# Encoder layer on one core: factor kept on chip, half product formed in PSUM, constants in one load, later sums for the second group, operands by halves

## The chip, the cores and the metric

The kernel runs on one core of a Trainium2 chip. The core has a matrix engine (TensorE, PE in the profile), a vector engine (VectorE, DVE), a scalar engine (ScalarE, ACT), GpSimd (POOL) and SyncE (SP), which here issues every DMA, in one queue and in order. Each engine runs its own instructions in the order of the program and waits for the others by semaphores. The metric is the time of one execution on the device in microseconds (us); lower is better.

## The reference

One encoder layer is computed in fp32 on a prompt of 512 tokens and a sample of 1024, with 1024 features: a feed-forward layer, a mixer (half long convolutions, half retention), and another feed-forward layer, each with norms before and after.

```python
def rmsnorm(x, g):
    return x * lax.rsqrt(jnp.mean(x * x, axis=-1, keepdims=True) + NORM_EPS) * g
def swiglu(h, w1, w3, w2):
    return (jax.nn.silu(h @ w1) * (h @ w3)) @ w2

x = x + 0.5 * rmsnorm(swiglu(rmsnorm(x, ffn1_pre_g), w1, w3, w2), ffn1_post_g)
u = rmsnorm(x, mix_pre_g) @ w_in
y_h = hyena_mixer(short_conv(u[..., :1536], short_w, short_b), ...)   # FFT convolutions, two orders
y_r = retention_mixer(u[..., 1536:], ...)
x = x + rmsnorm(concat(y_h, y_r) @ w_out, mix_post_g)
x = x + 0.5 * rmsnorm(swiglu(rmsnorm(x, ffn2_pre_g), w1, w3, w2), ffn2_post_g)
```

## The kernel before, in words

All 1536 tokens pass through each stage, with features on the partitions and tokens along the free axis. Every fp32 matrix product is three matmuls (`mm3`, L67 to L69): each operand is split into a high part, which ScalarE writes (`hi_act`, L59, tiles ending in h), and a low part, which VectorE subtracts (`lo`, L62, tiles ending in l); in the convolution GpSimd forms some of the low parts.

**Feed-forward layers** (0 to about 1050 us and from about 2210 us to the end). Tokens go in two groups g of 768, each in two halves th of 384. `quad` tiles hold 128 partitions x 4 blocks of features x 384 tokens (128x1536); kh is the half of the features. A scheme of seven products per unit takes the place of eight block products: `operands` forms b11, t2, b21, t3, t1, t4 and b22 from the four quarters of the normed input once for each group, and `up_unit`, called for 22 units f, multiplies weight sums with them into the banks ua, ub and uc. `normed` makes the normed input of a half: it loads xq, sums the squares (ScalarE squares, VectorE adds, L158 to L163), multiplies by the gains (L186), has TensorE sum over the partitions (`rstd3`, the bank ss, L172), spreads the factor r over the partitions (`spread`, three transposes into the bank rps, L179), and multiplies (L208). Where the factor is already known it takes another way: a row of factors in HBM is loaded with a broadcast (rq, L205). `post` of the mixer's closing computes that row (r, stored by L588), one `g` of 512 tokens at a time, for the second feed-forward layer.

The second group is made ready beside the units of the first. `ahead` is a generator whose steps the units call, one in the middle of each unit and one behind it: `normed` for both halves, stored to HBM (nx, L469), then sums of the down-projection's weights (`weight_sums`). A step of it contains several instructions, and its place in the program fixes the place of its matmuls in TensorE's order.

**The convolution** (`hyena`, 1715 to about 2125 us). `filter_spectra` transforms the filters (jobs K), `hyena` the signals (jobs Z): transposes into tr banks, `forward` into one bank fw for each block, then the product of the two spectra, complex and block by block, with s the filter's spectrum. It is these four lines, L989 to L992, for 48 blocks of 128x512:

```python
nc.vector.tensor_tensor(p1, ps, a, ALU.mult)
nc.vector.tensor_tensor(p2, ps, s[:, bi:bi + 1].broadcast_to([128, 2, 256]), ALU.mult)
nc.vector.tensor_tensor(p1[:, 0], p1[:, 0], p2[:, 1], ALU.add)
nc.vector.tensor_tensor(p1[:, 1], p1[:, 1], p2[:, 0], ALU.subtract)
```

ps is the fw bank in PSUM, p1 and p2 are in SBUF. ScalarE and GpSimd then split p1 into yh and yl, and the inverse transforms follow. Most jobs have two fw banks in turn (`alt`); the last three (pZ01, pZ10, pZ11) run beside the output projection with one.

**Constants.** `short_consts` loads the short convolution's three weights and its bias at the program's start, as 4 DMAs of single 4-byte elements (L868, L869).

The order of instructions on each engine comes from a scheduler that simulates a timeline when the program is built. The code's order and the generators' steps give it what it orders.

## Time and profile before

| | us |
|---|---|
| median of 3 runs | 3272.43 |
| the 3 runs | 3269.87, 3272.43, 6079.1 |
| the profiled execution | 3269.82 |
| its span in the trace | 3268.0 |
| TensorE busy in the span | 3044.8 (93%) |
| VectorE busy | 2621.3 (80%) |
| ScalarE busy | 1526.9 (47%) |
| GpSimd busy | 507.6 (16%) |

The profiled execution stands 1.8 us above its span and among the two lower runs. The run of 6079.1 is an outlier. Busy shares are averages over stages; idle time of an engine counts where that engine sets the pace of its stage. [...]

### The profile page before, as it was taken

To read this page: it belongs to the slowest core of one execution; us is meant where nothing else is said; L and a number is where in the kernel's file an instruction comes from. 1 tells how busy PE (TensorE), PEld (TensorE's weight loads), DVE (VectorE), ACT (ScalarE), POOL (GpSimd) and SP (SyncE) were. 2 spreads that over 40 slices of the span, in tenths; PEclk is the share of its full clock that TensorE was granted. 3 is DMA by queue.
4 is the path that set the end of the run, shared out by engine and by line. 5 is a ranking of instruction groups with operands and counts; after the bars stand their busy time and mean duration, and the time that the engine had idled before them with its cause. 6 is when DMAs were issued, how large, how long until landed. Compare 5 with 4: busy or idle time off the path is not lost. (4 is left out here: it accounts for less than half of the span.)

```text
span 3268.0 us, 46298 instructions
## 1 busy us (share of the span) xinstructions
PE 3044.8 (93%) x16766; PEld 2864.0 (88%) x16766; DVE 2621.3 (80%) x4215; ACT 1526.9 (47%) x2607; POOL 507.6 (16%) x368
## 2 busy tenths in 40 slices
PE   5999999999999999989989997996899999999997
PEld 4999999999999777767768886876899999999997
DVE  7888888877787599988767788887789788877776
ACT  6433465433455434457644344454433465433454
POOL 0000000000200112556424445520000000000000
PEclk9999999999999999999999998997899999999998
DMA  4686344422344634454652125474678344322244
GB/s 130 231 299 246 91 149 142 120 72 75 102 129 146 207 113 163 153 191 135 178 163 103 48 93 180 138 225 156 251 261 311 89 150 146 130 70 77 85 130 139
DMA packets 224181, 491.48 MB, mean 150 GB/s; under 512 B 37584, under 2 KB 65744, under 8 KB 221776
## 3 DMA queue, kind: packets, MB, share of 16 engines
q1 hardware_dynamic: 223952, 488.54, 46.0%
q8 instruction: 131, 2.15, 0.3%
q14 instruction: 98, 0.80, 0.1%
HBM read 386.67 MB, written 101.75 MB: 149 GB/s over the span
## 5 line engine op out<-in xcount | busy, mean ns | idle before, releaser
L68 PE MATMUL dn<-xl,w2h 128*128 128x384 f32 x1232 | 414.6, 337 | 6.4 <-DVE xl L62 6.4
L59 ACT ACTIVATE wh<-s 128x512 fp32r<-128x512 f32 x352 | 221.3, 631 | 412.9 <-PE ua L68 115.5
L67 PE MATMUL dn<-xh,w2h 128*128 128x384 f32 x1232 | 402.1, 336 | 1.8 <-ACT xh L59 1.7
L69 PE MATMUL dn<-xh,w2l 128*128 128x384 f32 x1232 | 401.8, 337 | 0.0
L59 ACT ACTIVATE wh<-raw 128x512 fp32r<-128x512 f32 (+1 forms) x316 | 220.7, 698 | 350.2 <-PE ub L68 93.5
L62 DVE TENSOR_TENSOR wl<-s,wh 128x512 fp32r<-128x512 f32 x352 | 241.3, 686 | 155.7 <-ACT wh L59 85.5
L59 ACT ACTIVATE w2h<-raw 128x512 fp32r<-128x512 f32 (+1 forms) x340 | 228.1, 672 | 269.7 <-PE dn L68 181.0
L96 POOL TENSOR_TENSOR r<-m,mhalf 128x3 f32<-128x3 f32 (+1 forms) x35 | 41.2, 1179 | 1904.0 <-DVE m L95 1903.1
L62 DVE TENSOR_TENSOR w2l<-raw,w2h 128x512 fp32r<-128x512 f32 (+1 forms) x320 | 225.7, 715 | 93.3 <-ACT w2h L59 78.0
L67 PE MATMUL wips<-hh,wh 128*128 128x512 f32 x576 | 230.8, 401 | 13.1 <-DVE o L812 6.3
L68 PEld LDWEIGHTS dn<-xl,w2h 128*128 128x128 f32 x1232 | 232.3, 189 | 7.2 <-DVE xl L62 7.1
L67 PEld LDWEIGHTS dn<-xh,w2h 128*128 128x128 f32 x1232 | 230.6, 188 | 2.3 <-ACT xh L59 2.0
L69 PE MATMUL wips<-hh,wl 128*128 128x512 f32 x576 | 229.7, 400 | 1.8 <-POOL wl L62 1.7
L69 PEld LDWEIGHTS dn<-xh,w2l 128*128 128x128 f32 x1232 | 231.3, 189 | 0.0
L68 PE MATMUL wips<-hl,wh 128*128 128x512 f32 x576 | 229.5, 399 | 0.0
L62 DVE TENSOR_TENSOR wl<-raw,wh 128x512 fp32r<-128x512 f32 (+1 forms) x280 | 201.4, 719 | 30.7 <-ACT wh L59 29.0
L67 PE MATMUL fw<-th,mh 128*128 128x256 f32 x448 | 132.9, 298 | 26.1 <-DVE spec L951 21.6
L67 PEld LDWEIGHTS wips<-hh,wh 128*128 128x128 f32 x576 | 110.2, 191 | 41.4 <-DVE o L812 6.3
L67 PE MATMUL ub<-t2h,wh 128*128 128x384 f32 x352 | 120.6, 343 | 25.1 <-ACT t2h L59 20.6
L67 PE MATMUL ub<-t4h,wh 128*128 128x384 f32 x352 | 121.2, 344 | 14.9 <-DVE u L279 14.1
L69 PEld LDWEIGHTS wips<-hh,wl 128*128 128x128 f32 x576 | 110.0, 191 | 28.4 <-POOL wl L62 3.1
L68 PE MATMUL fw<-tl,mh 128*128 128x256 f32 x448 | 133.2, 298 | 1.3 <-DVE tl L62 1.2
(386 smaller groups left out, 9075.9 us busy)
## 6 DMA issues: line engine op xcount, KB each, us to landing
raw<-ffn_w SPq DMA_DIRECT2D x440, 256.0 KB, 2.7
raw<-ws SPq DMA_DIRECT2D x220, 256.0 KB, 2.6
wsum<-ffn_w SPq DMA_DIRECT2D x60, 768.0 KB, 6.5
raw<-w_in_f SPq DMA_DIRECT2D x52, 512.0 KB, 4.1
ws<-wsum SPq DMA_DIRECT2D x30, 768.0 KB, 4.6
xq<-x SPq DMA_DIRECT2D x16, 768.0 KB, 5.8
res<-x SPq DMA_DIRECT2D x16, 768.0 KB, 6.0
wsum<-ffn_w SPq DMA_DIRECT2D x20, 512.0 KB, 6.6
```

The source lines that it names most:

```text
L59: self.nc.scalar.activation(hi, src, AF.Copy)
L62: eng.tensor_tensor(lo, src, hi.bitcast(F32), ALU.subtract)
L67: mm(ps, lhsT=ah, rhs=bh, start=first, stop=False, **kw)
L68: mm(ps, lhsT=ah, rhs=bl, start=False, stop=False, **kw)
L69: mm(ps, lhsT=al, rhs=bh, start=False, stop=last, **kw)
L96: nc.gpsimd.tensor_tensor(r, m, self.mhalf[:, :n], ALU.pow)
```

## The change

It has five parts.

1. `short_consts`: the host lays weights and bias side by side as `short`, and one DMA of 128 rows of 48 elements loads them.
2. `ahead`: behind the first step of `normed` (load, squares, sums) of each half of the second group, two more empty steps are yielded. The step with ss comes two half units later, and all steps behind it too.
3. `post`: the factor r is copied to a tile `near` of 128x8 in SBUF; only group 0 still stores its row. `ready` passes `near[:, 3:6]` to `normed` for the second half of the second layer's first group, and `normed` then spreads it by transposes.
4. `normed` multiplies by halves of the features (128x768), the two halves of the features in turn; `operands` forms t1 and t2 by halves, and b11 and t2 are split by halves. t1 is formed behind the load of h22.
5. `hyena`: p2 is formed first; then ps is multiplied by a in place, in PSUM; the add and the subtract read ps and p2 and write p1.

```diff
--- before.py
+++ after.py
@@ -75,6 +75,7 @@
         nc.sync.dma_start(self.ident, self.io["ident"])
         self.mhalf = self.cp.tile([128, 8], F32, name="mhalf")
         nc.gpsimd.memset(self.mhalf, -0.5)
+        self.near = self.cp.tile([128, 8], F32, name="near")
         self.one = ones = self.cp.tile([128, 1], F32, name="ones")
         nc.gpsimd.memset(ones, 1.0)
         self.ones = self.cp.tile([128, 128], F32R, name="onesr")
@@ -201,14 +202,23 @@
             r = self.spread(r)
         else:
             self.gained(xs, gi)
-            r = self.half("rq")
-            nc.sync.dma_start(r, row.broadcast_to([128, 384]))
+            if row.shape[0] == 128:
+                r = self.spread(row)
+            else:
+                r = self.half("rq")
+                nc.sync.dma_start(r, row.broadcast_to([128, 384]))
         yield
-        for x in xs:
-            nc.vector.tensor_tensor(x, x, r.unsqueeze(1).broadcast_to([128, 4, 384]), ALU.mult)
-
-    def split(self, pool, src, name):
+        for k in range(0, 4, 2):
+            for x in xs:
+                nc.vector.tensor_tensor(x[:, k:k + 2], x[:, k:k + 2], r.unsqueeze(1).broadcast_to([128, 2, 384]), ALU.mult)
+
+    def split(self, pool, src, name, halves=False):
         h, l = self.quad(pool, f"{name}h", F32R), self.quad(pool, f"{name}l", F32R)
+        if halves:
+            for k in range(0, 4, 2):
+                self.hi_act(h[:, k:k + 2], src[:, k:k + 2])
+                self.lo(self.nc.vector, l[:, k:k + 2], src[:, k:k + 2], h[:, k:k + 2])
+            return h, l
         self.hi_act(h, src)
         self.lo(self.nc.vector, l, src, h)
         return h, l
@@ -221,13 +231,14 @@
         b = first or {}
         h11, h12 = load(0, 0), load(0, 1)
         if not first:
-            b["11"] = self.split(X, h11, "b11")
+            b["11"] = self.split(X, h11, "b11", True)
         t1 = self.quad(Y, "t1")
-        tt(t1, h12, h11, ALU.subtract)
         yield
         h22, t2 = load(1, 1), self.quad(Y, "t2")
-        tt(t2, h22, t1, ALU.subtract)
-        b["t2"] = self.split(X, t2, "t2")
+        for k in (slice(0, 2), slice(2, 4)):
+            tt(t1[:, k], h12[:, k], h11[:, k], ALU.subtract)
+            tt(t2[:, k], h22[:, k], t1[:, k], ALU.subtract)
+        b["t2"] = self.split(X, t2, "t2", True)
         tt(h12, h22, h12, ALU.subtract)
         yield
         h21 = load(1, 0)
@@ -433,7 +444,7 @@
             return True
 
         def ready(g, th, xs):
-            row = None if row_in is None or g else row_in[:, 384 * th:384 * th + 384]
+            row = None if row_in is None or g else self.near[:, 3:6] if th else row_in[:, :384]
             return self.normed([srcs[g][kh][th] for kh in range(2)], pre, Y, row, xs)
 
         h = [], []
@@ -452,7 +463,7 @@
                     for step in steps:
                         next(step)
                 run(steps[0], 9)
-                first = {"11": self.split(X, h[0][0], "b11")}
+                first = {"11": self.split(X, h[0][0], "b11", True)}
                 run(steps[1], 9)
                 for _ in self.operands(lambda kh, th: h[th][kh], X, Y, first=first):
                     pass
@@ -464,7 +475,11 @@
                 yield from lead
                 for th in range(2):
                     xs = []
-                    yield from ready(1, th, xs)
+                    for i, _ in enumerate(ready(1, th, xs)):
+                        yield
+                        if i == 0:
+                            yield
+                            yield
                     for kh in range(2):
                         nc.sync.dma_start(nx[kh][th], xs[kh])
                     yield
@@ -585,7 +600,9 @@
             for t in range(4):
                 nc.tensor.matmul(ss[:, t:t + 1], lhsT=a2[:, t * 128:(t + 1) * 128], rhs=self.one, start=True, stop=True)
             r = self.rstd(ss, 1.0 / D)
-            nc.sync.dma_start(row[:, 512 * g:512 * g + 512].rearrange("o (c p) -> (o p) c", p=128), r)
+            nc.vector.tensor_copy(self.near[:, 4 * g:4 * g + 4], r)
+            if g == 0:
+                nc.sync.dma_start(row[:, 512 * g:512 * g + 512].rearrange("o (c p) -> (o p) c", p=128), r)
 
     def last_third(self, g, d, src, dst, X, Y):
 
@@ -863,10 +880,7 @@
             yield
 
     def short_consts(self):
-        nc = self.nc
-        for i in range(3):
-            nc.sync.dma_start(self.scw[:, :, i], self.io["short_w"][i])
-        nc.sync.dma_start(self.scw[:, :, 3], self.io["short_b"])
+        self.nc.sync.dma_start(self.scw, self.io["short"])
 
     def mix_in_consts(self, rop):
         self.rope = rop.tile([128, 2, 1024], F32, name="rope", bufs=1)
@@ -986,10 +1000,10 @@
             p2 = ca.tile([128, 2, 256], F32, tag="p2", name="p2", bufs=2)
             a = s[:, 0:2] if last else s[:, 0:1].broadcast_to([128, 2, 256])
             bi = 2 if last else 1
-            nc.vector.tensor_tensor(p1, ps, a, ALU.mult)
             nc.vector.tensor_tensor(p2, ps, s[:, bi:bi + 1].broadcast_to([128, 2, 256]), ALU.mult)
-            nc.vector.tensor_tensor(p1[:, 0], p1[:, 0], p2[:, 1], ALU.add)
-            nc.vector.tensor_tensor(p1[:, 1], p1[:, 1], p2[:, 0], ALU.subtract)
+            nc.vector.tensor_tensor(ps, ps, a, ALU.mult)
+            nc.vector.tensor_tensor(p1[:, 0], ps[:, 0], p2[:, 1], ALU.add)
+            nc.vector.tensor_tensor(p1[:, 1], ps[:, 1], p2[:, 0], ALU.subtract)
             pl = self.c1
             yh = pl.tile([128, 2, 256], F32R, tag=f"yh{i}", name="yh")
             yl = pl.tile([128, 2, 256], F32R, tag=f"yl{i}", name="yl")
@@ -1408,7 +1422,7 @@
     w=g('w_in').reshape(8,128,28,128).transpose(2,1,0,3)
     r['w_in_f']=asc(np.concatenate([w[:20],w[24:]]))
     r['w_in_v']=asc(g('w_in')[:,2560:3072].reshape(4,2,128,512).transpose(0,2,1,3))
-    r['short_w']=asc(g('short_w').reshape(3,12,128).transpose(0,2,1)); r['short_b']=asc(g('short_b').reshape(12,128).T)
+    r['short']=asc(np.concatenate([g('short_w'),g('short_b')[None]]).reshape(4,12,128).transpose(2,1,0))
     for i in '123': r['filt_w'+i]=g('filt_w'+i); r['filt_b'+i]=asc(g('filt_b'+i)[:,None])
     r['filt_freq']=asc(g('filt_freq')[:,None])
     r['filt_w4']=asc(g('filt_w4').reshape(64,16,128).transpose(1,0,2))
```

SyncE's queue at the program's start, before: ident and gains are the identity and the norms' gains, xq a quad of the input, raw a tile of weights, scw the short convolution's constants.

```order
L83 DMA gains<-gains 128x48
L194 DMA xq<-x 128x1536 x2
L250 DMA raw<-ffn_w 128x512 x5
L868 DMA scw<-short_w 128x12x1 x3
L869 DMA scw<-short_b 128x12x1
L194 DMA xq<-x 128x1536 x2
```

After, the same piece:

```order
L84 DMA gains<-gains 128x48
L195 DMA xq<-x 128x1536 x2
L261 DMA raw<-ffn_w 128x512 x5
L883 DMA scw<-short 128x48
L195 DMA xq<-x 128x1536 x2
```

One DMA stands in the place of four, between the first weights and the second half's input.

TensorE in the second feed-forward layer, around the ss of the second group's first half, before: it stands at the border of two units, behind b22, the last of a unit's seven products.

```order
L67 MATMUL uc<-b22h,wh 128x384
L68 MATMUL uc<-b22l,wh 128x384
L69 MATMUL uc<-b22h,wl 128x384
L172 MATMUL ss<-ones,acc 128x1 x3
L67 MATMUL ua<-b11h,wh 128x384
L68 MATMUL ua<-b11l,wh 128x384
L69 MATMUL ua<-b11h,wl 128x384
```

After:

```order
L67 MATMUL ub<-t3h,wh 128x384
L68 MATMUL ub<-t3l,wh 128x384
L69 MATMUL ub<-t3h,wl 128x384
L67 MATMUL uc<-t1h,wh 128x384
L68 MATMUL uc<-t1l,wh 128x384
L173 MATMUL ss<-ones,acc 128x1 x3
L69 MATMUL uc<-t1h,wl 128x384
```

The products with b11, t2, b21 and t3 of the next unit and two matmuls of t1 now stand ahead of ss, 50 matmuls in all; in the first layer it is five products, 60 matmuls.

SyncE's queue at the second feed-forward layer's start, before: row is the row of factors in HBM, z a piece of the output projection's result.

```order
L194 DMA xq<-x_000_82 128x1536
L194 DMA xq<-x_010_84 128x1536
L194 DMA xq<-x_001_83 128x1536
L194 DMA xq<-x_011_85 128x1536
L588 DMA row_91<-r 128x4x1
L624 DMA z_155<-z_21992 128x512
L250 DMA raw<-ffn_w 128x512
L205 DMA rq<-row_91 128x384
L250 DMA raw<-ffn_w 128x512 x8
```

After:

```order
L195 DMA xq<-x_000_83 128x1536
L195 DMA xq<-x_010_85 128x1536
L195 DMA xq<-x_001_84 128x1536
L195 DMA xq<-x_011_86 128x1536
L641 DMA z_156<-z_22023 128x512
L261 DMA raw<-ffn_w 128x512 x9
```

The store of the row and the load of its factors are gone from between the input, the z and the weights.

## Rows read from the trace of the kernel before

**Rows 1.** The page's first part: busy time, share and instructions by engine.
```profile
PE 3044.8 (93%) x16766; PEld 2864.0 (88%) x16766; DVE 2621.3 (80%) x4215; ACT 1526.9 (47%) x2607; POOL 507.6 (16%) x368
```

**Rows 2.** Stretches: length, busy us by engine (instructions), granted clock, DMA share, GB/s.
```profile
1715.00:2125.00 410.00, 365.43 (x2509) 336.58 (x2510) 331.31 (x538) 164.77 (x312) 189.39 (x156) 0.95 0.33 113
2208.00:2260.00 52.00, 25.33 (x100) 21.27 (x99) 37.24 (x44) 26.39 (x38) 3.46 (x2) 0.68 0.38 111
2360.00:3220.00 860.00, 856.82 (x4943) 855.20 (x4943) 685.83 (x1154) 395.41 (x699) 2.98 (x2) 1.00 0.46 146
```

**Rows 3.** Timeline of the start: start, duration, instruction, and the idle time before it.
```profile
5.36 6.16 SPq L868 DMA_DIRECT2D scw<-short_w  x3
...
17.25 1.48 ACT L158 ACTIVATE sq<-xq 128x1536 f32<-128x1536 f32 x1 [3.05 <-DMA xq<-x]
...
43.60 0.69 PE L67 MATMUL ub<-t2h,wh 128*128 128x384 f32 x1 [5.13 <-ACT t2h L59]
```

**Rows 4.** Timeline around the later sums of squares, both feed-forward layers, TensorE and ScalarE.
```profile
79.65 0.99 PE L172 MATMUL ss<-ones,acc 128*128 128x1 f32 x6 [4.21 <-DVE acc L162]
...
2294.98 1.48 ACT L158 ACTIVATE sq<-xq 128x1536 f32<-128x1536 f32 x1 [5.84 <-DMA xq<-x]
...
2306.92 1.44 PE L172 MATMUL ss<-ones,acc 128*128 128x1 f32 x6 [6.01 <-DVE acc L162]
...
2308.69 0.52 PE L68 MATMUL ua<-b11l,wh 128*128 128x384 f32 x1
...
2309.01 0.52 PE L69 MATMUL ua<-b11h,wl 128*128 128x384 f32 x1
...
2312.13 0.63 ACT L59 ACTIVATE wh<-raw 128x512 fp32r<-128x512 f32 x1 [5.39 <-PE ua L68]
...
2344.62 1.41 PE L172 MATMUL ss<-ones,acc 128*128 128x1 f32 x6 [3.75 <-DVE acc L162]
```

**Rows 5.** Timeline of the second feed-forward layer's start, SyncE's queue, VectorE, TensorE.
```profile
2214.63 0.37 SPq L588 DMA_DIRECT2D row<-r  x1
...
2219.98 0.32 SPq L624 DMA_DIRECT2D z<-z  x1
...
2230.21 0.69 DVE L270 TENSOR_TENSOR s<-s,raw 128x512 f32<-128x512 f32 x1 [4.70 <-DMA z<-z]
...
2232.82 1.76 DVE L208 TENSOR_TENSOR xq<-xq,rq 128x1536 f32<-128x1536 f32 x1 [1.85 <-ACT wh L59]
...
2244.96 0.69 PE L67 MATMUL ub<-t2h,wh 128*128 128x384 f32 x1 [15.52 <-ACT t2h L59]
```

**Rows 6.** DMA issues between 2160 and 2240 us: count, KB each, us to landing.
```profile
row<-r SPq DMA_DIRECT2D x2, 2.0 KB, 14.5
```

**Rows 7.** VectorE's groups by line and shape: busy us, mean ns, idle before.
```profile
L279 DVE TENSOR_TENSOR u<-ub,p 128x384 f32<-128x384 f32 x88 | 48.9, 556 | 52.9 <-PE ub L69 52.6
...
L991 DVE TENSOR_TENSOR p<-p,p 128x256 f32<-128x256 f32 x48 | 34.7, 723 | 0.8
...
L992 DVE TENSOR_TENSOR p<-p,p 128x256 f32<-128x256 f32 x48 | 31.9, 665 | 0.0
...
L405 DVE TENSOR_TENSOR z<-z,rps 128x768 f32<-128x768 f32 x32 | 28.4, 947 | 3.0 <-PE rps L179 3.0
```

**Rows 8.** The tile of the products: durations in ns, shortest/median/longest.
```profile
L990 DVE TENSOR_TENSOR p<-fw,spec x48: 669/674/681, 1755.1 to 2117.4; 128x512 f32<-128x512 f32 x48
L991 DVE TENSOR_TENSOR p<-p,p x48: 403/458/2612, 1756.3 to 2121.7; 128x256 f32<-128x256 f32 x48
L992 DVE TENSOR_TENSOR p<-p,p x48: 406/414/2654, 1756.6 to 2122.1; 128x256 f32<-128x256 f32 x48
```

**Rows 9.** Timeline of one half product in the convolution, VectorE beside GpSimd.
```profile
1829.36 1.29 POOL L62 TENSOR_TENSOR yl<-p,yh 128x512 fp32r<-128x512 f32 x1 [1.42 <-ACT yh L59]
...
1829.79 1.14 DVE L991 TENSOR_TENSOR p<-p,p 128x256 f32<-128x256 f32 x1
```

**Rows 10.** TensorE's waits in the convolution, 1715 to 2125 us: total, times, longest.
```profile
PE fw L67 <- DVE spec L951: 21.6, 17, 3.5
```

## The prediction

> **What bounds the kernel now.** The page's first part comes first: TensorE is busy 3044.8 of 3268.0 us [rows 1]. It can give back 223 us at most, and only where it stands still or runs below its clock. The table of stretches then says where: the long run of the second feed-forward layer leaves 3 us of 860 idle, at a granted clock of 1.00, while the convolution (1715 to 2125 us) leaves 44.6 of 410 and the second layer's start (2208 to 2260) 26.7 of 52, at a clock of 0.68 [rows 2]. The program's first 46 us were read in the timeline, and in the long runs only the waits that stand out. The change touches four such places. The profiled execution took 3269.82 us, 1.8 more than its span; the runs of before that agree lie at 3269.87 and 3272.43, so the sum below, made against 3269.8, holds for the median to within 3 us.
>
> **Part 1, the constants' load.** Three DMAs with elements of 4 bytes keep SyncE's queue for 6.16 us [rows 3], and the load of the second half's input is issued behind them. ScalarE's square of that input stands 3.05 us for it. One DMA with rows of 192 bytes takes the place of four (the new order shows it in the same spot). ScalarE's chain can start earlier by those 3.05 us and no more, since ScalarE itself is busy up to then; the new splitting by halves lets the first b-operand start sooner, but TensorE's wait of 5.13 us before the product with t2 ends on a chain of VectorE and ScalarE that only moves along with its start. I take 2.7 us. Bounds: 0, if the transfer is as late as now, and 4.5, if the halves also take 1.5 off the wait of 5.13.
>
> **Part 2, sums of squares later.** In both layers TensorE reaches a small matmul (ss) before VectorE has its operand: 4.21 us in the first layer, 6.01 and 3.75 in the second [rows 4], 13.97 together. Behind each stands a stretch at half clock. After 2306.92 the matmuls of 384 columns follow each other every 0.32 us [rows 4], where the long run does 4943 in 856.82 us, 0.173 each [rows 2]. I count one product of 12 matmuls at that clock behind each of the three, 3 x 12 x (0.32 - 0.173) = 5.3, and twice 0.4 for the small matmuls, which take 1.44 and 1.41 us there and 0.99 in the first layer. That makes 6.1 on top of the waits, 20.1 in all. In the new order ss stands 50 to 60 matmuls further on, 50 x 0.173 = 8.7 us and 60 x 0.173 = 10.4. The longest wait is 6.01, so the operand would be there. What else could stop TensorE in that time? ScalarE prepares the weights, and after the second layer's ss it waited 5.39 us for TensorE to free a buffer [rows 4]; so the weights were ahead, and ScalarE follows when TensorE goes on. Against it speaks that ScalarE itself stood 5.84 us for the input, with conversions of weights queued behind. A part of the wait may appear again there. I take 15 of the 20.1. Bounds: 0 and 20.1. The steps behind ss (factor, multiply, two stores to HBM, the weight sums) are later by two half units; the stores are read back only in the other group, hundreds of us on, and of the 37 steps that fit ahead of unit 19 the list takes 32 and 34 in the two layers in place of 28 and 30, so none is pushed to the end.
>
> **Part 3, the factor stays on chip.** At the second layer's start SyncE issues the factor's store at 2214.63, the store of a z at 2219.98 [rows 5]. The first takes 14.5 us to land [rows 6], and the loads behind it land late as well: VectorE stood 4.70 us for the z store (it releases the buffer that the weight sum L270 writes), then ran the multiply by the loaded factor at 2232.82, and TensorE waited 15.52 us for t2 [rows 5]. In the new kernel this store and the load of the factor are gone for the last group; one copy of 128x4 and three transposes take their place. The order moves the z store and the weight loads right behind the input's loads. The z store would then land some 4 us after its issue, near 2224, L270 could run at 2227, the two factor multiplies no longer wait, and the halves give ScalarE the first half of t2 near 2236. That is TensorE's product with t2 at 2236 in place of 2244.96. But TensorE then runs into VectorE's queue again: from 2224 on VectorE has b11's low part (1.8), four half multiplies (0.947 each [rows 7]), t1 and t2 (1.75 each as whole), four low parts of weights (0.7 each) and the low parts of t2, b21 and t3 (1.75 each), and only the waits among these can go: 4.70 and 1.85 [rows 5]. I take 6.0 of the sum 6.55. Halves cost VectorE little: 0.947 against 0.88, half of 1.76, so 0.07 for each of some ten pairs, 1.4 us in both layers, beside work that waits anyway. Bounds: 0 (something else of DMA holds L270's buffer as long) and 15.5, the whole wait.
>
> **Part 4, the half product in PSUM.** The last two operations of each block read two tiles of SBUF. Their shortest takes 403 and 406 ns, their mean is 723 and 665 and their longest 2.6 us; the product before them, with one operand in PSUM, takes 669 to 681 in all 48 [rows 7, 8]. 34.7 - 48 x 0.403 = 15.4 and 31.9 - 48 x 0.406 = 12.4: 27.8 us are stretch. A stretched one ends just after a GpSimd operation that it overlaps, here at 1829.79 + 1.14 = 1830.93 where GpSimd ended at 1829.36 + 1.29 = 1830.65 [rows 9]. With one operand in PSUM the two would be of the kind that did not stretch. Their bare length I take from other reads of PSUM: 556 ns at 384 columns [rows 7] and 674 at 512 [rows 8], so 438 at 256; against 403 and 406 that is 0.03 x 96 = 3.2 us more. VectorE gains 27.8 - 3.2 = 24.6 us, over 410. TensorE gains only where it waits for VectorE: 21.6 us for the filters' spectra [rows 10], which stand in VectorE's queue among these products, and some smaller waits. Against it, the bank with the block's spectrum is released after the fourth operation and not after the second. That is 2 x 0.44 = 0.88 us later, and TensorE's next block in that bank waits where no other bank is free. No row shows VectorE writing PSUM: its price is bounded by 0 extra (as the reads cost nothing that stretches) and by a doubling, 0.67 x 48 = 32 us; I take 0, as the reads of PSUM at 384 columns are 0.006 off those of SBUF. How much of 24.6 reaches TensorE? Of the waits for spectra I count half, 11, and take off 3 for the bank held in the jobs that have only one bank. Net 8. Bounds: a gain of 25, and a loss of 74 (the bank held 0.88 us longer in each of 48 blocks, 42, and the doubled write, 32).
>
> [...]
>
> **The sum.** 2.7 + 15 + 6 + 8 = 31.7; 3269.8 - 31.7 = 3238.
>
> **The rivals.**
> (a) The wait of part 2 only moves. If ScalarE's 5.84 us for the input [rows 4] is what the conversions behind it pay, TensorE stops a product later for about as long, at half clock again, and of 15 only 3 come: 3250 (3244 to 3262). For it: the conversions of weights that TensorE needs next stand in ScalarE's queue behind that square. Against it: the 5.39 us of ScalarE idle after.
> (b) The other side, slower than before. The write into PSUM is slow and the bank is held: TensorE stands 0.88 us in each of 48 blocks, 42 us, and where the write doubles too, another 32. With the other parts' 23.7 that is 3288 to 3320. It decides from 0.5 us a block on (24 / 48). For it: the convolution has its spectrum in few banks, and TensorE already waits there. Against it: of the 44.6 us idle, half are waits for the filters, which use none of this.
> (c) Part 4 does not do what it says: the multiply in place and the adds stretch as well, since one of their operands still stands in SBUF beside GpSimd's; then its 8 are gone: 3246 (3242 to 3254).
> (d) More than forecast in the convolution: nearly all waits for VectorE vanish, 24.6 in place of 8: 3221 (3214 to 3226).
>
> **How the numbers follow.** The forecast (3226 to 3252 as its own range) 0.53, (a) 0.17, (b) 0.08, (c) 0.10, (d) 0.12. The range from 3216 to 3264 holds the forecast, (a), (c) and most of (d), and leaves out (b). A time 2% off, 65 us (what a measurement here can tell from no change), needs all four parts at the ends of their bounds (4.5 + 20.1 + 15.5 + 25 = 65), or more than (b) at its worst: 0.02 each side.
>
> **What would show it.** In the changed kernel's profile: no wait at ss after 60 us, and full clock there; ss reached with its operand ready. No store of the factor near 2214, and the product with t2 at 2237 or so. The two operations at 0.41 to 0.45 us with a longest under 0.5. ScalarE's square at 14 us without a wait. The forecast is wrong if TensorE's waits for fw grow past 21.6 us, or if the wait of 6 us stands again before another product.

## The result, and the profile after

The changed kernel takes 3231.14 us in the median of 4 runs (3224.18 to 3233.14), the kernel before 3269.87 in the median of the 3 beside it (the run of 6079.1 us is left out; with it the median of 4 is 3271.15). The ratio is 0.988, with a 95% interval of 0.9865 to 0.9896: 39 us faster. The forecast was 3238, with a range from 3216 to 3264. The profiled execution of the changed kernel took 3229.38 us, its span is 3227.6.

Where the 40 us of the two spans lie is read from the same instruction in both timelines (start of it, in us; a unit ends with its last matmul with b22, and in the second layer's first unit 3 matmuls more stand ahead of it in the new order, 0.5 us; the difference grows over most of the stages):

| landmark on TensorE | before | after | ahead by |
|---|---|---|---|
| first product (ua) | 34.29 | 31.26 | 3.0 |
| first down-projection (dn), first layer | 381.59 | 367.09 | 14.5 |
| first matmul of the mixer (v) | 1059.06 | 1046.37 | 12.7 |
| first block of the convolution (fw) | 1717.35 | 1702.61 | 14.7 |
| last inverse transform (b) | 2133.15 | 2117.51 | 15.6 |
| last output projection (proj) | 2215.85 | 2196.32 | 19.5 |
| second layer, end of the first unit | 2270.42 | 2242.56 | 27.9 |
| second layer, end of the eighth unit | 2396.22 | 2353.31 | 42.9 |
| last transposes (rps) | 3257.00 | 3216.37 | 40.6 |

Two stretches carry 35 of the 40 us: the units of the first layer's first group (11.5), and the start and first units of the second layer (23.4). The convolution itself brings 0.9 us.

The stretches of the changed kernel that answer to [rows 2] (length, busy us by engine with instructions, granted clock as a share of full speed, DMA share, GB/s):

```profile
1715.00:2115.00 400.00, 362.65 (x2480) 332.23 (x2479) 298.69 (x539) 160.15 (x303) 190.47 (x156) 0.96 0.32 109
2200.00:2250.00 50.00, 35.56 (x163) 33.25 (x164) 47.40 (x66) 29.54 (x44) 1.65 (x1) 0.73 0.32 105
2340.00:3180.00 840.00, 836.40 (x4825) 834.41 (x4824) 675.26 (x1135) 387.42 (x686) 2.98 (x2) 1.00 0.48 156
```

Here the second layer's start has TensorE busy for 35.6 of 50 us where it was 25.3 of 52. VectorE is 33 us less busy over the whole program (2588.3 us where it was 2621.3 [rows 1]), 28 of them between the first fw and the last b. In the convolution TensorE stands still for 37 us of 400 where it did for 45 of 410: a share of 9% against 11%.

The start, as in [rows 3] (SyncE, ScalarE, TensorE):

```profile
5.40 0.54 SPq L883 DMA_DIRECT2D scw<-short  x1
...
14.04 1.47 ACT L159 ACTIVATE sq<-xq 128x1536 f32<-128x1536 f32 x1
...
39.32 0.69 PE L67 MATMUL ub<-t2h,wh 128*128 128x384 f32 x1 [3.88 <-ACT t2h L59]
```

One DMA of 0.54 us has taken the place of 7.0 us in the queue. ScalarE's square of the second half's input begins at 14.04 with no wait, 3.2 us earlier, and the wait before the product with t2 is 3.88 in place of 5.13.

TensorE's waits over the whole program (us in total, times, longest), with [rows 4] and [rows 10] in mind:

```profile
PE ss L173 <- DVE acc L163: 31.0, 5, 15.2
...
PE fw L67 <- DVE spec L965: 12.6, 16, 2.6
...
PE fw L67 <- DVE p L1006: 9.1, 6, 2.6
```

Before, the first and the last of them were

```profile
PE ss L172 <- DVE acc L162: 48.0, 8, 15.2
...
PE fw L67 <- DVE p L990: 4.3, 6, 1.5
```

The waits for the sums of squares are 31.0 us in 5 places; before they were 48.0 in 8. The three that are gone are those of [rows 4]; the five left are the program's start, where another 3 us went, and other norms. For the blocks of the convolution the wait for the spectra fell from 21.6 to 12.6 [rows 10], and the wait for the product, which now ends with the fourth operation, grew from 4.3 to 9.1.

The second layer's start, as in [rows 5] (SyncE, VectorE, TensorE, ScalarE):

```profile
2200.55 0.32 SPq L641 DMA_DIRECT2D z<-z  x1
...
2196.01 0.17 DVE L603 COPY near<-r 128x4 f32<-128x4 f32 x1
...
2205.90 0.68 DVE L281 TENSOR_TENSOR s<-s,raw 128x512 f32<-128x512 f32 x1
...
2206.58 0.95 DVE L213 TENSOR_TENSOR xq<-xq,rps 128x768 f32<-128x768 f32 x1
...
2211.87 0.66 PE L67 MATMUL ua<-b11h,wh 128*128 128x384 f32 x1 [8.88 <-DVE xq L213]
...
2213.84 0.84 ACT L59 ACTIVATE t2h<-t 128x768 fp32r<-128x768 f32 x1 [3.69 <-DVE t L240]
...
2222.21 0.69 PE L68 MATMUL ua<-b21l,wh 128*128 128x384 f32 x1 [2.37 <-DVE b21l L62]
```

The factor is copied at 2196.01, no store of it follows, the z store goes out at 2200.55, and L281, which needs it, runs at 2205.90 with no wait; before, the same weight sum stood 4.70 us. The first half of t2's high part is formed at 2213.84. What is late instead is seen in TensorE's rows: it now waits 8.88 us before its first product, for VectorE's multiply, and 2.37 for a low part. VectorE is the bound of this stretch, 47.4 of 50 us.

The four operations of a product of spectra (ns shortest/median/longest), as in [rows 8], the in-place multiply after them:

```profile
L1003 DVE TENSOR_TENSOR p<-fw,spec x48: 673/680/694, 1738.8 to 2102.5; 128x512 f32<-128x512 f32 x48
L1005 DVE TENSOR_TENSOR p<-fw,p x48: 406/412/425, 1740.6 to 2104.9; 128x256 f32<-128x256 f32 x48
L1006 DVE TENSOR_TENSOR p<-fw,p x48: 406/411/415, 1740.9 to 2105.2; 128x256 f32<-128x256 f32 x48
```

```profile
L1004 DVE TENSOR_TENSOR fw<-fw,spec x48: 680/689/690, 1739.4 to 2103.1; 128x512 f32<-128x512 f32 x48
```

No operation is stretched any more: the longest of the add and the subtract is 425 and 415 ns where it was 2.6 us. The write into PSUM takes 689 ns against 680 for the same operation into SBUF (medians). The add and the subtract take 412 and 411 ns in the median with one operand in PSUM; with both in SBUF their shortest before was 403 and 406 [rows 8].

### The profile page after: what moved, and what is told of

The parts are those of the page before. It is cut to its first block, busy times and chain, and to the rows that moved or that the text cites. A ratio compares the mean times of both kernels' runs of the same rounds, so it can differ in the third digit from the quotient of the medians.

```text
span 3227.6 us, 46280 instructions
## 1 busy us (share of the span) xinstructions
PE 3036.5 (94%) x16769; PEld 2855.2 (88%) x16769; DVE 2588.3 (80%) x4249; ACT 1526.8 (47%) x2615; POOL 504.9 (16%) x368
## 5 line engine op out<-in xcount | busy, mean ns | idle before, releaser
L62 DVE TENSOR_TENSOR wl<-raw,wh 128x512 fp32r<-128x512 f32 (+1 forms) x280 | 203.2, 726 | 22.1 <-ACT wh L59 19.5
L67 PE MATMUL fw<-th,mh 128*128 128x256 f32 x448 | 133.8, 300 | 21.8 <-DVE spec L965 12.6
L68 PEld LDWEIGHTS wips<-hl,wh 128*128 128x128 f32 x576 | 109.4, 190 | 24.8
```

The costliest lines, as they stand in the source:

```text
L62: eng.tensor_tensor(lo, src, hi.bitcast(F32), ALU.subtract)
L67: mm(ps, lhsT=ah, rhs=bh, start=first, stop=False, **kw)
L68: mm(ps, lhsT=ah, rhs=bl, start=False, stop=False, **kw)
```

## The experiments

Each of the five parts was run alone on the kernel before, and two taken out of the changed kernel. The kernel before was run beside each; its medians in the four sittings were 3269.87, 3266.66, 3270.90 and 3274.63 us, so only ratios are compared across sittings. In the list of the change the halves are part 4 and the product in PSUM part 5; the prediction has no part of its own for the halves, and its part 4 is the product.

| run | ratio to before | 95% interval | us of 3270 |
|---|---|---|---|
| the whole change | 0.9880 | 0.9865 to 0.9896 | -39 |
| later sums alone | 0.9928 | 0.9910 to 0.9946 | -24 |
| factor on chip alone | 0.9983 | 0.9971 to 0.9995 | -6 |
| product in PSUM alone | 1.0009 | 0.9997 to 1.0022 | +3 |
| one load of constants alone | 1.0004 | 0.9993 to 1.0016 | +1 |
| halves alone | 0.9970 | 0.9958 to 0.9981 | -10 |
| change without halves | 0.9892 | 0.9879 to 0.9906 | -35 |
| change without product in PSUM | 0.9883 | 0.9866 to 0.9901 | -38 |
| weight sums alone four steps later | 0.9984 | 0.9975 to 0.9994 | -5 |
| factor on chip, row still stored | 0.9992 | 0.9982 to 1.0002 | -3 |
| change with one empty step for two | 0.9908 | 0.9891 to 0.9926 | -30 |
| before, yl on VectorE | 0.9988 | 0.9978 to 0.9997 | -4 |
| before, no add and subtract | 1.0020 | 1.0011 to 1.0029 | +7 |

### Later sums alone

```diff
-                    yield from ready(1, th, xs)
+                    for i, _ in enumerate(ready(1, th, xs)):
+                        yield
+                        if i == 0:
+                            yield
+                            yield
```

> The kernel before with part 2 alone (two more empty steps behind the sums of squares of the second group). My theory, by the trace of the changed kernel: the three waits at ss (4.21, 6.01, 3.75) and the half clock behind them go and little comes back, so 18 to 24 us faster, 3246 to 3252. By the prediction's term: 15. Rival (the wait only moves to ScalarE's input): at most 6 us faster, and a new wait of some 5 us before a product within 10 us of the old place.

It gave 24 us, the upper end of what was expected and more than the prediction's 15. In its profile TensorE's waits for the sums are

```profile
PE ss L172 <- DVE acc L162: 34.5, 5, 15.3
```

and no wait of their size stands behind them: between 62 and 390 us TensorE stands still for 0.7 us in all, before it was 9.8, and in the second layer the longest new wait is 1.72 us, for a low part of weights at 2287.80. The rival, that the wait only moves, falls.

### Weight sums later, sums of squares as before

The wait of 4.24 us that the first 400 us of the kernel before have beside the 4.21 at ss is this one, on TensorE:

```profile
177.75 0.69 PE L67 MATMUL ub<-t2h,wh 128*128 128x384 f32 x1 [4.24 <-ACT wh L59]
```

```diff
+                for _ in range(4):
+                    yield
                 yield from self.weight_sums(w2, Y)
```

> The kernel before with only the weight sums four steps later (as they are in part 2) and the sums of squares where they were. Part 2 alone gave 24 us where its three waits and the half clock behind them were counted at 20. In its trace a fourth wait is gone too: 4.24 us at 177.75, before a product with t2, for a conversion of weights in ScalarE's queue, in the time of the weight sums. Theory: this one goes with the later weight sums: 4 to 6 us faster, and the three waits at ss stay at 4 to 6 us each. Rival: it goes only when ss is later too (the steps behind ss); then 0 us and the wait near 178 stays.

It was 5 us faster, and the wait near 178 is gone while the one at ss stays:

```profile
81.08 1.41 PE L172 MATMUL ss<-ones,acc 128*128 128x1 f32 x6 [4.80 <-DVE acc L162]
```

So part 2 has a second effect, which comes from where it pushes the weight sums. With the 20.1 us of the three waits this makes 25, about what part 2 gave alone.

### One empty step in place of two

```diff
                         if i == 0:
                             yield
-                            yield
```

> The changed kernel with one empty step in place of two behind the sums of squares. A step is half a unit, some 42 matmuls, 7.2 us at 0.172; the longest wait was 6.01. Theory: one step is nearly enough, the waits at ss are 0 to 2 us and the time within 4 us of the changed kernel, 3228 to 3236. Rival (the operand itself comes later when TensorE runs on, since VectorE's and ScalarE's queues hold the units' work ahead of it): waits of 3 us and more come back, 8 us slower or more.

9 us of the gain were lost (the two intervals just overlap), so the rival holds. The profiled execution is the slowest of the six, 3255.19 us with a median of 3243.65, so its waits may be longer than in the others. One wait at ss is still 2.52 us, and the other has become a wait of 8.04 us in ScalarE's queue (ScalarE, then TensorE):

```profile
2330.42 1.48 ACT L159 ACTIVATE sq<-xq 128x1536 f32<-128x1536 f32 x1 [2.06 <-DMA xq<-x]
...
2335.35 0.47 ACT L279 ACTIVATE p<-ua 128x384 f32<-128x384 f32 x1
...
2335.87 0.69 PE L67 MATMUL ua<-b21h,wh 128*128 128x384 f32 x1 [8.04 <-ACT p L279]
```

ScalarE's copy p of the bank ua stands behind the squares and gains of the second half's input, and TensorE's next product into ua stands behind that copy. With two steps TensorE has no wait of this kind: in the changed kernel its longest between 2240 and 2400 us is 2.4 us, for VectorE's u.

### The factor on chip alone, and with its store kept

```diff
-        row = None if row_in is None or g else row_in[:, 384 * th:384 * th + 384]
+        row = None if row_in is None or g else self.near[:, 3:6] if th else row_in[:, :384]
```

(with the copy to near and the transposes of the change's diff)

> The kernel before with part 3 alone (factor kept on chip, the last group's row neither stored nor loaded), multiplies and splits whole as before. My theory: the z store lands early, VectorE's waits of 4.70 and 1.85 us go, and the second layer's first product with t2 starts 5 to 7 us earlier: 5 to 7 us faster. Rival: the gain of the second layer's start in the changed kernel (8 us between the end of the output projection and the end of the first unit) came from the halves; then this one alone gives under 3 us.

```diff
-            if g == 0:
+            if True:
                 nc.sync.dma_start(row[:, 512 * g:512 * g + 512].rearrange("o (c p) -> (o p) c", p=128), r)
```

> Part 3 alone, but the last group's row of factors is still stored to HBM, though nobody reads it. Part 3 alone gave 5.3 us. Theory one (the store of 4-byte elements keeps the transfers behind it, the z store above all, as long as 14 us): with the store back VectorE waits 4 to 5 us for z again and at most 2 us of the gain stay. Theory two (the load of the factor was what VectorE waited for): 4 to 6 us faster as without the store.

Alone it gave 5.5 us; with the store kept, 2.6, an interval that just reaches zero and overlaps the other. The stretch from the last output projection to the end of the first unit was 54.6 us before, 47.8 with the part alone, 51.2 with the store kept: in these traces half of the 6.8 comes from leaving out the store and half from the rest of the part, in which the load of the factor is gone. In the run with the store it stands ahead of z and of the weights in SyncE's queue (SyncE, VectorE, TensorE):

```profile
2221.42 0.37 SPq L594 DMA_DIRECT2D row<-r  x1
...
2237.08 0.69 DVE L274 TENSOR_TENSOR s<-s,raw 128x512 f32<-128x512 f32 x1 [5.61 <-DMA raw<-ffn_w]
...
2241.99 0.66 PE L67 MATMUL ua<-b11h,wh 128*128 128x384 f32 x1 [12.82 <-DVE xq L212]
```

VectorE's weight sum waits 5.61 us, and TensorE's first product 12.82 us. The weight sum needs both the z store, which releases its buffer, and a load of weights; the trace names the load, but the two land within 0.3 us of each other, and the z store took 11.0 us to land where it took 3.4 without the row's store. So theory one's wait for z is back, and 2.6 us of the gain stay where at most 2 were expected. In the run without the store TensorE's wait is 7.51:

```profile
2232.54 0.66 PE L67 MATMUL ua<-b11h,wh 128*128 128x384 f32 x1 [7.51 <-DVE xq L212]
```

### The constants in one load, alone

```diff
-        for i in range(3):
-            nc.sync.dma_start(self.scw[:, :, i], self.io["short_w"][i])
-        nc.sync.dma_start(self.scw[:, :, 3], self.io["short_b"])
+        self.nc.sync.dma_start(self.scw, self.io["short"])
```

> The kernel before with part 1 alone (one load of the constants). Theory: ScalarE's wait of 3.05 us for the second half's input goes, the first product starts 3.0 us earlier, and that carries to the end: 2 to 4 us faster. Rival: the wait of TensorE before the product with t2 ends on other work and takes it back: 0 to 1 us.

In its trace the end of the first unit is 3.3 us earlier and still 3.1 at the first down-projection. In the medians nothing is clear of zero at the end. The trace does not explain that: its first down-projection takes 165.2 us where the kernel before takes 162.1, by a slower pace of TensorE (228 matmuls in the 40 us from 400 on, where the kernel before does 233), which loses the 3.1; but the mixer's first matmul is again 2.4 us earlier, and the last transposes are 5.1 earlier. What takes the gain in the medians stays open.

### The halves, alone and taken out

```diff
-        for x in xs:
-            nc.vector.tensor_tensor(x, x, r.unsqueeze(1).broadcast_to([128, 4, 384]), ALU.mult)
+        for k in range(0, 4, 2):
+            for x in xs:
+                nc.vector.tensor_tensor(x[:, k:k + 2], x[:, k:k + 2], r.unsqueeze(1).broadcast_to([128, 2, 384]), ALU.mult)
```

(and b11, t1 and t2 likewise; the second run is the changed kernel with all of this taken back)

> The kernel before with part 4 of the change's list alone (multiply, b11, t1 and t2 by halves of the features). The parts measured alone so far sum to some 29 us, the whole change to some 36 to 40. Theory one (the rest is the halves'): 4 to 8 us faster, with the product with t2 earlier by 1.5 us at the program's start and by 2 to 4 at the second layer's. Theory two (the rest comes from parts together: the halves help only once the factor is on chip): 0 to 2 us faster alone, since the second half's multiply still waits for the loaded factor.

> The changed kernel with whole multiplies and splits. Theory one: 4 to 8 us slower than the changed kernel, 3235 to 3239. Theory two: about as much or a little more, and then the halves alone gave nothing. Rival (the halves cost as much VectorE time as they give): 3229 to 3233, as the changed kernel.

Alone 9 to 10 us faster, taken out 4 us slower (0.9892 against 0.9880, and the intervals overlap). Theory one is nearest in number but has the wrong place. At the places that the halves touch they gave nothing: alone, the 84th matmul of the units (one unit's worth) starts 26.0 us after the first where it was 26.2, and in the second layer 50.9 us after the last output projection where it was 50.4. The whole gain of its trace lies between the convolution's first block and the last output projection: 486.2 us in place of 498.5. No line of that stretch was edited. What differs there is the order of instructions: counted row by row in the traces, 600 of the 2912 matmuls of that stretch stand otherwise, presumably because the scheduler simulates the whole program. TensorE's waits in it fell from 46 to 36 us, most of that before transposes (tr) that wait for VectorE's low part tl (9.7 us before, 0.9 here). That the order is the cause is likely and not shown: four other kernels whose order there is that of the kernel before (constants alone; and, with one matmul and two VectorE operations more, factor alone, factor with the row stored, change without the product in PSUM) took 493.1 to 497.7 us. So one order gives values 5.4 us apart from profile to profile, and 6.9 of the 12.3 lie beyond that.

### The product in PSUM: alone, taken out, and what bounds it

```diff
-            nc.vector.tensor_tensor(p1, ps, a, ALU.mult)
+            nc.vector.tensor_tensor(ps, ps, a, ALU.mult)
-            nc.vector.tensor_tensor(p1[:, 0], p1[:, 0], p2[:, 1], ALU.add)
-            nc.vector.tensor_tensor(p1[:, 1], p1[:, 1], p2[:, 0], ALU.subtract)
+            nc.vector.tensor_tensor(p1[:, 0], ps[:, 0], p2[:, 1], ALU.add)
+            nc.vector.tensor_tensor(p1[:, 1], ps[:, 1], p2[:, 0], ALU.subtract)
```

(p2 is formed ahead of the in-place multiply; the second run is the changed kernel with this taken back)

> The kernel before with part 4 alone (product in place in PSUM). The changed kernel's trace has VectorE's two operations at 0.41 us with no long ones, yet the convolution there is only 1 to 2 us shorter. Theory one (the bank held longer eats it): VectorE some 33 us less busy, TensorE's waits for fw by the spectra down by 9 us and by the product up by 5, time 1 to 4 us faster. Theory two (prediction): 8 us faster, and the rest of the changed kernel hid it.

> The changed kernel with the half product formed in SBUF as before. Alone the part gave nothing (0.09% slower, not clear of zero). Theory one (bank held longer takes what the spectra get): within 3 us of the changed kernel, 3228 to 3234, with TensorE's wait for fw by the spectra near 21 us and by the product near 4. Prediction's term: 8 us slower, 3239.

Alone it is 0.09% slower, not clear of zero (from 1 us faster to 7 slower); taken out it leaves the change at 0.9883. The part gives nothing that can be measured in the time. Alone, TensorE's waits in the convolution for the spectra and for the product are

```profile
PE fw L67 <- DVE spec L951: 15.3, 15, 3.0
...
PE fw L67 <- DVE p L992: 8.5, 6, 2.6
```

where they were 21.6 [rows 10] and 4.3. In the changed kernel without the part they are

```profile
PE fw L67 <- DVE spec L965: 19.9, 17, 3.3
...
PE fw L67 <- DVE p L1004: 4.4, 6, 1.5
```

and with it 12.6 and 9.1. So the waits for the spectra do fall with the part, by 6.3 us alone and 7.3 in the change, and 4.2 and 4.7 go into the bank held longer: 2.1 and 2.6 us are left on TensorE, of VectorE's 30 (alone it is busy 2591.4 us). The change without the part came out as theory one expected.

Two runs go further. The first asks whether GpSimd stretches the two operations:

```diff
-            self.lo(nc.gpsimd, yl, p1, yh)
+            self.lo(nc.vector, yl, p1, yh)
```

> The kernel before, with the low part yl of the product formed by VectorE in place of GpSimd. Theory (GpSimd's own work on SBUF stretches VectorE's operations with two SBUF operands): the add and the subtract take 0.40 to 0.42 us, means under 0.45, though both operands are still in SBUF; a few long ones stay beside GpSimd's fold and gate. VectorE gets 48 x 0.69 = 33 us of work and loses 27 of stretch. Rival (the stretch belongs to the operands in SBUF whatever GpSimd does): means stay at 0.72 and 0.67. Time: within 10 us of before.

VectorE's add and subtract, both operands still in SBUF (busy us, mean ns):

```profile
L991 DVE TENSOR_TENSOR p<-p,p 128x256 f32<-128x256 f32 x48 | 28.6, 596 | 0.1
L992 DVE TENSOR_TENSOR p<-p,p 128x256 f32<-128x256 f32 x48 | 23.2, 483 | 0.0
```

Their shortest here takes 409 and 411 ns. Of the stretch of 27.8 us [rows 7, 8] 28.6 - 48 x 0.409 = 9.0 and 23.2 - 48 x 0.411 = 3.5 are left, 12.5. More than half went with GpSimd's work; means under 0.45 were expected, and they are not. The overlaps in the two traces tell of the rest. In the kernel before 35 of the 96 operations took more than 0.45 us, and each of them overlaps a GpSimd operation; of the 61 short ones 6 overlap one by more than 0.1 us. Here 7 are still long, up to 2.6 us, and each overlaps one of GpSimd's other operations, which were left in place (folds, low parts of weights w2l, the result y); of the 89 short ones 2 do. So the stretch of these operations belongs to GpSimd's work beside them.

The second was to bound the worth of any relief:

```diff
-            nc.vector.tensor_tensor(p1[:, 0], p1[:, 0], p2[:, 1], ALU.add)
-            nc.vector.tensor_tensor(p1[:, 1], p1[:, 1], p2[:, 0], ALU.subtract)
```

> The kernel before without the add and the subtract of the product of spectra: they are left out, so the convolution's output is not the reference's. VectorE has 67 us less to do there, and the bank of the block is released after the second operation, as before. It bounds what any relief of VectorE in these lines can give. Theory one (part 4 gave VectorE 33 us and lost it to the bank held): TensorE's wait for fw by the spectra falls to 12 or less, by the product stays at 4 or less, and the convolution (first fw to last b) gets at least 10 us shorter than before's 415. Rival (VectorE's time there is not what TensorE waits for): less than 4 us shorter.

Stretch by stretch (the run, then the kernel before; PE, PEld, DVE busy):

```profile
1700.00:2130.00 430.00, 373.12 (x2540) 341.50 (x2539) 280.37 (x451) 170.43 (x320) 196.94 (x170) 0.94 0.35 119
```

```profile
1700.00:2130.00 430.00, 374.56 (x2551) 343.44 (x2550) 337.80 (x547) 170.25 (x319) 198.91 (x166) 0.94 0.34 118
```

VectorE has 57 us less to do, and from the first fw to the last b TensorE takes 414.9 us, before 415.8. The wait for the spectra did not fall, and the one for the product grew:

```profile
PE fw L67 <- DVE spec L951: 24.7, 19, 5.9
...
PE fw L67 <- DVE p L990: 7.6, 7, 3.7
```

By these numbers the rival holds, but the run does not bound the gain as it was meant to. The scheduler ordered it anew: 1279 of the 2912 matmuls up to the last output projection stand otherwise than in the kernel before (1415 in the part alone), and the program is 7 us slower with less work to do. No run here relieves VectorE in the old order, so what that would give is open.

What the waits for spectra are is told by the trace of the kernel before, by what VectorE did ahead of each. Two of the 17 (VectorE, then TensorE, twice):

```profile
1798.60 1.34 DVE L773 TENSOR_TENSOR fz<-fe 128x128 f32<-128x128 f32 x1
...
1800.07 1.65 DVE L951 SCALAR_TENSOR_TENSOR spec<-fw,turn,spec 128x256 f32<-128x256 f32 x4
...
1801.08 0.55 PE L67 MATMUL fw<-th,mh 128*128 128x256 f32 x1 [3.31 <-DVE spec L951]
...
1807.45 0.88 DVE L951 SCALAR_TENSOR_TENSOR spec<-fw,turn,spec 128x256 f32<-128x256 f32 x2 [5.73 <-ACT spec L949]
...
1808.47 0.35 PE L67 MATMUL fw<-th,mh 128*128 128x256 f32 x1 [0.84 <-DVE spec L951]
```

At 1800.07 the spectra come behind folds in VectorE's queue (fz and fe: sums and differences that prepare a signal for its transform), and TensorE waits 3.31 us. At 1807.45 VectorE has been idle for 5.73 us, waiting for ScalarE's part of the spectrum, and TensorE waits 0.84. Nine of the 17 waits are of the second kind, 5.5 us together: VectorE's load has no part in them. Eight are of the first, 16.1 us. Directly ahead of the spectra stands a fold in six of these (13.8 us) and a low part tl in two (2.3), never an operation of the product. In the run without add and subtract the folds still stand there: 15.6 of its 24.7 us are of the first kind, in the part alone, 8.7 of 15.3. So shorter products do shorten the first kind, by 7.4 us, through what stands behind them in the queue, and the second kind not at all.

## Why the prediction came out right, and where its steps did not

**The constants.** The step held at its place (3.0 us at the first product, 2.7 forecast) and did not show at the end: 0 in the medians, with 2.3 us faster as the interval's edge.

**The later sums.** The mechanism was right, the size was not: 24 us against 15. Only 15 of the 20.1 were counted, for a wait that would come back behind ScalarE's input, and that allowance was the error: none of that size came back, so the 20.1 us counted fit the result. Another 5 came from the wait at 177.75, which no term had: the sum went through the waits at ss only, and not through what else the same steps would move. The rival (a) was right about one step, as the run with one empty step shows, and two steps are past it.

**The factor on chip.** 6 forecast, 5.5 alone; in the whole change the stretch is 8.3 us shorter. The chain (store, z, VectorE) held; in the traces it is half of the gain, and the other half came with the load that is gone.

**The halves.** They were put at nothing on TensorE's path and a little VectorE time, and at their own places that is what was seen. Their 9 to 10 us alone stand in another stage, whose order of instructions changed. No term of the sum had that.

**The product in PSUM.** This is the step that failed: "Of the waits for spectra I count half, 11, and take off 3 for the bank held". VectorE's 24.6 us came as forecast (the add and the subtract took 66.6 us and take 39.6, 27 less), at the forecast length, and the write into PSUM cost 9 ns an operation. What was mis-sized is what reaches TensorE: the waits for spectra fell by 6.3 and not 11, the bank held took 4.2 and not 3, so 2.1 us were left of the forecast 8, and the time shows none of them. The row of the waits was read as one queue, with the products in it. In nine of the 17 waits, 5.5 us, nothing stood ahead of the spectra, since VectorE was waiting for ScalarE; in the other eight, 16.1 us, mostly folds did, so shorter products helped by 7.4 us. Why the 2.1 us do not show in the time is open; the part also changed the order of the stage.

For an operand in PSUM the forecast took 0.03 us more an operation. The traces show 5 to 9 ns more: medians of 412 and 411 ns with one operand in PSUM against the shortest of 403 and 406 with both in SBUF [rows 8]. The 27.8 us of stretch went when the second SBUF operand went (the longest is now 425 and 415 ns), and 15.3 of them went when yl alone moved from GpSimd to VectorE.

That the sum of the forecast, 31.7, came near the measured 39 is in part luck: two terms too high (8 for the product, 2.7 for the constants) and two too low (15, and nothing for the halves) partly cancelled. Alone the five parts add up to some 35.

## What to carry to other kernels

A wait that the trace puts down to VectorE can be a queue that is too long or a short chain behind another engine, and the same trace tells which: look at whether the engine was idle ahead of the operation that ends the wait, and at what stood there if it was not. Here 5.5 of 21.6 us were such a chain, and the rest stood directly behind folds and low parts; making another operation of that queue shorter took 7.4 us off it, less than half. A small matmul that waited in a long run cost its wait and a slower clock behind it: 6.01 us at 2306.92 in the kernel before, then a granted clock of 0.50 from 2307 to 2312 us, with a matmul every 0.32 us where the long run has 0.173. Moving this one and two others later, and the weight sums with them, gave 24 us, and no wait of their size stood in for them; with half the delay ScalarE's queue did, by a wait of 8.04 us, and 9 us of the gain were lost. Where a scheduler orders the whole program, an edit of one stage can change the order in another, and a run that leaves work out is then no clean bound. A part's worth is to be read at its own place as well as in the total, and beside what two profiles of one order differ by (here up to 5.4 us in one stage).

## What was not expected of the hardware

Two stretches of the same work in the kernel before, in its first and second pass of the first layer's down-projection, with TensorE busy all the time and a granted clock of 1.00:

```profile
400.00:440.00 40.00, 40.00 (x233) 40.00 (x231) 34.39 (x68) 25.74 (x55) 0.00 (x0) 1.00 0.45 124
920.00:960.00 40.00, 40.00 (x229) 40.00 (x228) 30.03 (x51) 23.03 (x41) 0.00 (x0) 1.00 0.44 127
```

233 matmuls in 40 us, and 229. The spacing is 0.172 us in the one and 0.175 in the other, over tens of us; in the same two stretches the run with the constants alone does 228 and 233, the slower pace first, and the changed kernel 233 in both. A pass has 924 matmuls, so this is worth 2.8 us, in work that no edit touched; the first pass took 162.1 us in the kernel before and 165.2 with the constants alone. That is as much as the first part of the change gave at its place. What sets the pace was not tried.
